# Hymba-style decoder layer, one core: where normalized columns leave from, when the t3 block is made, how many operands are loaded ahead

## The chip, the cores and the metric

One core of one Trainium2 chip runs the whole layer in one program. The metric is the device time of that program in microseconds (us), the median of several runs; lower is better. The engines are PE (matrix multiply, with PEld for its weight loads), DVE (VectorE), ACT (ScalarE), POOL (GpSimd) and SP, whose queue issues every DMA of the part spoken of here.

## What is computed

One decoder layer on 1024 tokens of width 1024, in float32. The change lies in its last half, the squared-ReLU MLP between two norms:

```python
x = x + jnp.concatenate([attn, conv], axis=-1) @ w_out[l]
h = rmsnorm(x, norm_ffn_g[l])
x = x + jnp.square(jax.nn.relu(h @ w_ffn_up[l])) @ w_ffn_down[l]
return rmsnorm(x, norm_final_g)
```

## The kernel before

Each float32 operand is split into a high part (ACT, L55) and a low part (DVE or POOL, L56), and a product is three passes of PE (L59 to L61). Each engine runs a queue of its own in order; outside the hand-ordered attention part the framework's scheduler sets the order of each queue, and each DMA is issued from SP's queue, on one of eight semaphores in turn. Tiles of one tag share a ring of buffers; who allocates the next one waits for the last readers and writers of the buffer that it gets.

**The second norm** (`norm_rows` and `norm_cols2`). For each of eight blocks of 128 tokens PE makes the last part of the output projection (`oc`), DVE adds it to the residual `x2[t]` (L815), SP stores `x2[t]` to `x2d` (L860), ACT squares and sums it into a buffer `xn` (L116), POOL makes the inverse root (L82, L83), DVE multiplies into `xn` (L145). One block later `norm_cols2` transposes `xn` on PE (L851, tile `n_t`), splits the columns into `h2h` and `h2l`, copies the columns once more on ACT (L854) and stores them to `hraw` in DRAM (L855). There are two `xn` buffers.

**The up projection.** Sixteen pairs of 128 hidden columns each. Pairs 0 and 1 are plain (`up_plain`): four products `up` of 24 matmuls over `h2h`/`h2l`, one for each half `e` of the columns and half `hf` of the tokens. Pairs 2 to 15 use seven products of half the size in place of eight (`up7`, tiles `u`), whose moving operands are sums of blocks of the columns: `t1s`, `t2s`, `t4s` (`make_moving`, from tiles `b` that are loaded back from `hraw`) and t3, the difference of two blocks of the second token half (`make_t3`, tiles `c`), which is written over the first four rows of `h2h[1]` and `h2l[1]`. The products of a pair run in the order 1, 5, 6, 2, 3, 7, 4. ACT copies the first two out of PSUM (L991, L992, tiles `us`); four PSUM tiles `two` go round. Results and their sums (`work_q`, `work_s`; L906, L907, L908, L914) are stored to `hid` in DRAM (L893).

**The down projection** has seven groups of seven products `dn` each, and an eighth whose products go straight into the final sums: group 0 takes the products in the order 1, 2, 3, 5, 6, 7, 4. A product needs a block of `hid` (tile `h`, one load) and a block of the weights (`b11`, `b21`, `b22`, `b12`, or the sums t1, t2 and b22 - b12 that POOL makes in `sums`), which `prep` splits into operands `d0..hi` and `d0..lo` (three buffers each). It has two halves of 12 matmuls; each half is added to an accumulator: `xe`, copied by ACT for group 0, or the residual `xr`, which is loaded back from `x2d` in four tiles (`reload_x2`). `xr0` takes the buffer of `work_q`, so its loads wait for the last store of the up projection. `begin_down`, in the middle of the last up pair, loads the operands of the first three products.

Of the kernel before, what the change touches and what calls it, by code (L numbers as in the profile page):

```python
# [5 lines left out]
F32 = mybir.dt.float32  # L6
F32R = mybir.dt.float32r
BF16 = mybir.dt.bfloat16
AF = mybir.ActivationFunctionType
# [5 lines left out]
P = 128  # L15
S = 1024
D = 1024
KT = D // P
# [9 lines left out]
HN = 512  # L28
# [5 lines left out]
def body(tc, x, norm_mix_g, w_in, b_forget, conv_dw_w, conv_dw_b, conv_ln_g, conv_ln_b,  # L34
# [3 lines left out]
    V, A, G, T, SP = nc.vector, nc.scalar, nc.gpsimd, nc.tensor, nc.sync  # L38
# [15 lines left out]
    def split(hi, lo, src, eng=V):  # L54
        A.activation(hi, src, AF.Copy)  # L55
        eng.tensor_tensor(lo, src, f32(hi), op=ALU.subtract)  # L56

    def mm3(ps, sh, sl, mh, ml, first, last):
        T.matmul(ps, sh, mh, start=first, stop=False)  # L59
        T.matmul(ps, sh, ml, start=False, stop=False)  # L60
        T.matmul(ps, sl, mh, start=False, stop=last)  # L61
# [7 lines left out]
    def ps_big(name):  # L69
        return psum.tile([P, 2 * HN], F32, tag="big", name=name, bufs=2)  # L70
# [666 lines left out]
    for t in range(NT):  # L737
        n = CV0 + CVS * t
# [23 lines left out]
    with tc.manual_schedule(engines={mybir.EngineType.PE}):  # L762
        for n in range(START, len(units) + 30):
# [4 lines left out]
            if 0 <= n < len(units):  # L768
                weighted_v(n, *prs.pop(n))
                h, hf, kt = units[n]  # L770
# [12 lines left out]
    x2 = [x2t[t // 2][:, t % 2, :] for t in range(NT)]  # L783
# [60 lines left out]
    hraw = dram.tile([KT, P, S], F32, name="hraw")  # L844
    x2d = dram.tile([NT, P, D], F32, name="x2d")

    def norm_cols2(t):
        xn = xns.pop(t)
        pt = ps_big(f"n2_{t}_t")
        for k in range(KT):  # L850
            T.transpose(pt[:, k * P:(k + 1) * P], xn[:, k * P:(k + 1) * P], ident)  # L851
        hf, c = t // 4, (t % 4) * P
        split(h2h[hf][:, :, c:c + P], h2l[hf][:, :, c:c + P], pt.rearrange("p (k n) -> p k n", k=KT))
        A.activation(xn, pt, AF.Copy)  # L854
        SP.dma_start(hraw[:, :, t * P:(t + 1) * P].rearrange("k p n -> p k n"), xn.rearrange("p (k n) -> p k n", k=KT))  # L855

    for t in range(NT):
        for hf in range(2):
# [6 lines left out]
    def ps_two(name):  # L865
        return psum.tile([P, 2, HN], F32, tag="two", name=name, bufs=4)
# [5 lines left out]
    def raw4(name):  # L872
        return rps[0].tile([P, 2, HN], F32, tag="raw4", name=name, bufs=8)

    def load_up(j):
        return load_w2(w_up_k[:, :, j * P:(j + 2) * P], f"up{j}", [P, KT, 2 * P])
# [7 lines left out]
    def up_half(p, w, e, hf, ps):  # L884
        sl = slice(e * P, (e + 1) * P)
        for k in range(KT):
            mm3(ps, w[0][:, k, sl], w[1][:, k, sl], h2h[hf][:, k, :], h2l[hf][:, k, :], k == 0, k == KT - 1)
        q = work["q"][:, e, hf, :]
        A.activation(q, ps, AF.Relu)
        V.tensor_tensor(q, ps, q, op=ALU.mult)  # L890

    def store(p, i, a):
        SP.dma_start(hid[i][p if i else p - NPAIR + 2], a)  # L893

    def sums_up(p, last):
        q, sm = work["q"], work["s"]
        a11, a21, a12, a22 = q[:, 0, 0, :], q[:, 0, 1, :], q[:, 1, 0, :], q[:, 1, 1, :]
        s1, s2, s3, s4 = [sm[:, i, :] for i in range(4)]
        plain = p >= NPAIR - 2
        if not last:  # L900
            store(p, 1, a11)
            store(p, 4, a22)
            if plain:
                store(p, 0, a21)
                return
            V.tensor_tensor(s1, a21, a22, op=ALU.add)  # L906
            V.tensor_tensor(s2, s1, a11, op=ALU.subtract)  # L907
            V.tensor_tensor(s3, a11, a21, op=ALU.subtract)  # L908
            for i, a in ((5, s1), (6, s2), (7, s3)):
                store(p, i, a)  # L910
        else:
            store(p, 2, a12)
            if not plain:
                V.tensor_tensor(s4, a12, s2, op=ALU.subtract)  # L914
                store(p, 3, s4)

    def up_plain(p, w, hfs):
        for e in range(2):
            for hf in hfs:
                up_half(p, w, e, hf, ps_two(f"up{p}{e}{hf}")[:, 0, :])  # L920
        sums_up(p, False)
        sums_up(p, True)

# [29 lines left out]
        mov[4] = [(t4[k // 2][:, k % 2, 0, :], t4[k // 2][:, k % 2, 1, :]) for k in range(4)]  # L953

    def tmp(name):
        return tp.tile([P, HN], F32, tag="tmp", name=name, bufs=6)

    def load_hraw(name, k, hf):
        t = tmp(name)
        SP.dma_start(t, hraw[k, :, hf * HN:(hf + 1) * HN])  # L960
        return t
# [10 lines left out]
    def make_t3(k):  # L972
        b12, b22 = load_hraw(f"c12_{k}", k, 1), load_hraw(f"c22_{k}", 4 + k, 1)
        G.tensor_tensor(b12, b22, b12, op=ALU.subtract)
        split(*mov[7][k], b12)
# [31 lines left out]
    SEQ0 = (1, 2, 3, 5, 6, 7, 4)  # L1007
# [6 lines left out]
    def wtile(g, name, dt=F32):  # L1014
        if "wr" not in pools_d:
            return raw4(f"{name}_{g}")
        return pools_d["wr"].tile([P, 2, HN], dt, tag="wr", name=f"{name}_{g}", bufs=9)

    def load_b(g, nm):
        e, c = BLK[nm]  # L1020
        d = groups.setdefault(g, {})
        wd = w_dn_k[:, 4 * g:4 * g + 4, :].rearrange("p (q e) n -> p e q n", e=2)
        d[nm] = wtile(g, "b" + nm)
        SP.dma_start(d[nm], wd[:, e, :, c * HN:(c + 1) * HN])

    def load_h(g, i):
        d = groups.setdefault(g, {})
        d[i] = raw4(f"h{i}_{g}")
        src = hid[i][2 * g:2 * g + 2] if i else hid[0]
        SP.dma_start(d[i], src.rearrange("q p n -> p q n"))  # L1030
# [20 lines left out]
    def pair_tiles(name):  # L1051
        return [wgt.tile([P, 2, 2, HN], F32R, tag=tg, name=f"{name}{tg}", bufs=3) for tg in ("hi", "lo")]

    def prep(g, i):
        d = groups[g]
        hi, lo = pair_tiles(f"d{g}{i}")
        w = d["w"][i] if "w" in d else d[{1: "11", 2: "21", 3: "22"}[i]]
        if i == 4:
            G.tensor_tensor(w, d["21"], w, op=ALU.subtract)
        split(hi[:, 0], lo[:, 0], d[i])  # L1060
        split(hi[:, 1], lo[:, 1], w, G if i in (1, 2) else V)
        return hi, lo

    NPL = 2
    uws = {0: load_up(0)}
# [7 lines left out]
    tp = pool("tp", "left")  # L1073
# [5 lines left out]
    def begin_down():  # L1079
        vp0.release()  # L1080
        vp1.release()
        rps.append(pool("rp", "right"))
        for nm, i in (("11", 1), ("21", 2), ("22", 3)):
            load_b(0, nm)
            load_h(0, i)
        ready[0] = prep(*steps[0])

    for p in range(NPAIR):
        if p + 1 < NPAIR:
            uws[p + 1] = load_up(2 * p + 2) if p + 1 < NPL else load_up7(p + 1)  # L1090
        if p < NPL:
            for k in range(2 * p, 2 * p + 2):
                make_moving(k)
            up_plain(p, uws.pop(p), range(2) if p else (1,))
        else:
            if p == NPL:
                for k in range(4):
                    make_t3(k)
            up7(p, uws.pop(p), begin_down if p == NPAIR - 1 else None)
    tp.release()  # L1100
    hp.release()
# [1 line left out]
    xp = pool("xp", "left")  # L1103
# [3 lines left out]
    x2 = []  # L1107
# [35 lines left out]
    for n in range(-1, len(steps)):  # L1143
        if n < 0:
            ready[1] = prep(*steps[1])
            load_b(0, "12")
            load_h(0, SEQ0[3])
            reload_x2(0)
            reload_x2(1)
            load_h(0, SEQ0[4])  # L1150
            reload_x2(2)
            reload_x2(3)
            for i in SEQ0[5:]:
                load_h(0, i)
            sums(0)
            continue
        g, i = steps[n]
        if n == 3:
            for h in range(2):
                V.tensor_tensor(acc_of(3, h), acc_of(3, h), acc_of(5, h), op=ALU.subtract)  # L1160
        if n % 7 == 4 and g + 1 < NG - 1:
            sums(g + 1)
        if n + AHEAD < len(steps):
            ready[n + AHEAD] = prep(*steps[n + AHEAD])
        if i == 1:
            load_group(g + 1)
        if n == len(steps) - 1:
            d = groups[NG - 1]
            ops = {}
            for x, y, name in ((1, "11", "sa"), (2, "21", "sb"), ("12", "22", "sc"), (0, 4, "sd")):  # L1170
                if name == "sc":
                    hi, lo = [[wtile(NG - 1, f"{name}{e}{k}", F32R) for k in range(2)] for e in "hl"]
                else:
                    hi, lo = pair_tiles(name)
                    hi, lo = [hi[:, 0], hi[:, 1]], [lo[:, 0], lo[:, 1]]
                for k, z in enumerate((x, y)):
                    split(hi[k], lo[k], d[z])
                    ops[z] = hi[k], lo[k]
        products(g, i, *ready.pop(n))

    fin = xp.tile([P, D], F32, name="gfin")
    SP.dma_start(fin, norm_final_g.partition_broadcast(P))

    def final(t):
        y = wgt.tile([P, D], F32, tag="raw", name=f"yo{t}", bufs=3)
# [56 lines left out]
```

## Time and profile before

| | us |
|---|---|
| median of 3 runs | 1184.75 |
| lowest and highest | 1181.86, 1185.16 |
| profiled execution, its own time | 1181.96 |
| its span in the trace | 1180.2 |
| PE busy in the span | 1128.8 (96%) |
| DVE, ACT, POOL busy | 905.4 (77%), 466.2 (40%), 461.1 (39%) |
| HBM traffic over the span | 138 GB/s |

A busy time counts an engine's instructions, not the waits between them. PE's clock is granted at one of two levels, and the mean of a stretch is given as a share of the higher one. A wait is put down to what ended it. A line such as L851 is a line of the kernel before.

### The profile page before, as it was taken

How to read it: one execution, taken by the hardware profiler on the slowest of the kernel's cores; microseconds unless marked ns; L12 is line 12 of the kernel's file. 1: busy time of each engine (PE TensorE's matmuls, PEld its weight loads, DVE VectorE, ACT ScalarE, POOL GpSimd, SP SyncE). 2: the span in 40 equal slices, each digit the busy share in tenths (PEclk: the TensorE clock that was granted, in tenths of full speed). 3: DMA queues.
4: the chain of work that ended last, by engine and by line, in shares of the span. 5: the costliest groups of instructions: out<-in, count | busy, mean ns of one | idle time of the engine just before them, and what ended most of it. 6: DMA issues, size and time to landing. Idle time of an engine off the chain costs nothing.

```text
span 1180.2 us, 15131 instructions
## 1 busy us (share of the span) xinstructions
PE 1128.8 (96%) x5455; PEld 918.7 (78%) x5455; DVE 905.4 (77%) x1155; ACT 466.2 (40%) x715; POOL 461.1 (39%) x358
## 2 busy tenths in 40 slices
PE   6999999989999999989799999999979999999997
PEld 6899888867677678867688888888858888888876
DVE  5399999577887764555887878787568888878994
ACT  6322443138788932353322222222324433333422
POOL 7113255027778520134543434433264333443011
PEclk9999999999999999998899999999989999999999
DMA  8021145773333243355544444444684554445003
GB/s 265 11 67 46 27 108 133 203 210 108 91 91 90 101 167 110 122 179 181 202 137 167 134 161 147 151 154 164 250 335 155 178 169 141 137 147 173 19 17 126
DMA packets 121779, 164.52 MB, mean 139 GB/s; under 512 B 9112, under 2 KB 66792, under 8 KB 121704
## 3 DMA queue, kind: packets, MB, share of 16 engines
q1 hardware_dynamic: 121704, 163.56, 43.4%
q8 instruction: 43, 0.70, 0.3%
q14 instruction: 32, 0.26, 0.1%
HBM read 114.67 MB, written 48.79 MB: 138 GB/s over the span
## 4 chain that ended last, share of the span: by engine, by line
PE 56%; DVE 7%; ACT 4%; issue 3%; DMA 3%; POOL 2%; SPq 0%; DVEq 0%; POOLq 0%; ACTq 0%
PE u L59 7%; PE u L60 7%; PE u L61 7%; PE dn L60 7%; PE dn L61 7%; PE dn L59 7%; DMA hraw<-n_xn 2%; PE op L59 1%; PE op L61 1%; PE op L60 1%; DVE xr L1138 1%; PE fin L59 1%; PE fin L61 1%; PE fin L60 1%; PE s L445 1%
## 5 line engine op out<-in xcount | busy, mean ns | idle before, releaser
L292 DVE SCALAR_TENSOR_TENSOR conv<-u,par,conv 128x1024 f32<-128x1024 f32 x108 | 133.7, 1279 | 1.7 <-ACT conv L287 1.3
L1138 DVE TENSOR_TENSOR xr<-dn,xr 128x1024 f32<-128x1024 f32 x56 | 68.0, 1219 | 35.9 <-PE dn L61 35.8
L56 POOL TENSOR_TENSOR pl<-pt,ph 128x512 fp32r<-128x512 f32 (+3 forms) x71 | 74.1, 1059 | 25.1 <-ACT ph L55 22.0
L935 POOL TENSOR_TENSOR ur<-ur 128x512 f32<-128x512 f32 x14 | 22.7, 1620 | 93.4 <-DVE ulo6a L56 7.4
L613 ACT ACTIVATE pt<-sT,ctok 128x512 f32<-128x512 f32 (+1 forms) x96 | 54.5, 585 | 10.9 <-PE sT L611 5.8
L989 DVE SCALAR_TENSOR_TENSOR work_q<-work_q 128x512 f32<-128x512 f32 x56 | 52.7, 942 | 1.0
L453 DVE CUSTOM_DVE_ANT_0 mj<-s,ck 128x512 bf16<-128x512 f32 (+2 forms) x64 | 37.4, 585 | 19.8 <-PE s L447 8.8
L988 DVE TENSOR_TENSOR work_q<-u,us 128x512 f32<-128x512 f32 x42 | 28.6, 681 | 26.9 <-PE u L61 26.9
L55 ACT ACTIVATE ph<-pt 128x512 fp32r<-128x512 f32 (+1 forms) x96 | 48.7, 531 | 0.6
L1138 DVE TENSOR_TENSOR xe<-dn,xe 128x1024 f32<-128x1024 f32 x36 | 42.8, 1212 | 4.0 <-PE dn L61 4.0
L82 POOL TENSOR_SCALAR rs_tmp<-n_ss 128x1 f32<-128x1 f32 x16 | 5.6, 353 | 94.8 <-ACT n_xn L116 88.1
L59 PE MATMUL qk<-hTh,wh_qk 128*128 128x512 f32 x96 | 39.0, 406 | 0.4 <-DVE m L453 0.4
L60 PE MATMUL qk<-hTl,wh_qk 128*128 128x512 f32 x96 | 37.9, 395 | 0.0
L61 PE MATMUL qk<-hTh,wl_qk 128*128 128x512 f32 x96 | 37.8, 394 | 0.0
L445 PE MATMUL s<-ks,q 128*128 128x512 f32 (+2 forms) x96 | 36.8, 389 | 1.0 <-DVE m L453 0.9
L633 PE MATMUL av<-pl,v 128*65 128x512 f32 (+1 forms) x96 | 32.5, 339 | 3.9 <-POOL pl L56 2.4
L61 PE MATMUL v<-wh_v,hTl 128*128 128x260 f32 x128 | 36.1, 282 | 0.0
L60 PE MATMUL v<-wl_v,hTh 128*128 128x260 f32 x128 | 36.1, 282 | 0.0
L59 PE MATMUL v<-wh_v,hTh 128*128 128x260 f32 x128 | 36.0, 281 | 0.0
L631 PE MATMUL av<-ph,v 128*65 128x512 f32 (+1 forms) x96 | 35.3, 368 | 0.1
L930 POOL TENSOR_TENSOR ur<-ur 128x512 f32<-128x512 f32 x14 | 24.5, 1750 | 25.3 <-DVE up2l L56 2.5
L608 PE MATMUL sT<-q,ks 128*128 128x512 f32 (+1 forms) x96 | 33.6, 350 | 0.0
(1315 smaller groups left out, 3897.8 us busy)
## 6 DMA issues: line engine op xcount, KB each, us to landing
h<-hid SPq DMA_DIRECT2D x53, 512.0 KB
b<-in_w_ffn_down SPq DMA_DIRECT2D x32, 512.0 KB
ur<-in_w_ffn_up SPq DMA_DIRECT2D x56, 256.0 KB
hid<-work_s SPq DMA_DIRECT2D x56, 256.0 KB
hid<-work_q SPq DMA_DIRECT2D x50, 256.0 KB
xp<-in_x SPq DMA_DIRECT2D x8, 512.0 KB
qstack<-qk SPq DMA_DIRECT2D x32, 128.0 KB
kstack<-qk SPq DMA_DIRECT2D x32, 128.0 KB
```

What stands on the lines that cost most here:

```text
L55: A.activation(hi, src, AF.Copy)
L56: eng.tensor_tensor(lo, src, f32(hi), op=ALU.subtract)
L59: T.matmul(ps, sh, mh, start=first, stop=False)
L60: T.matmul(ps, sh, ml, start=False, stop=False)
L61: T.matmul(ps, sl, mh, start=False, stop=last)
L292: V.scalar_tensor_tensor(dst, u[:, k:k + S], tap_w(c, k), cell[0], op0=ALU.mult, op1=ALU.add)
L445: T.matmul(ps[:, :w], d["q2"][:, i * P:(i + 1) * P], d["ks"][:, b0:b1], start=True, stop=b1 < n)
L453: V.tensor_tensor_reduce(junk[:, :w], ps[:, :w], d["ck"][:, b0:b1], op0=ALU.subtract, op1=ALU.max, scale=1.0, scalar=d.pop("m0") if b0 els ...
L613: A.activation(pt[:, :w], ps[:, :w], AF.Exp, bias=ctok[:, h * NT + kt:h * NT + kt + 1])
L631: T.matmul(av[:DH + 1, o0:], v1, ph[:, :w], start=kt == ORDER[hf][0], stop=False)
L989: V.scalar_tensor_tensor(dst, dst, 0.0, dst, op0=ALU.max, op1=ALU.mult)
L1138: V.tensor_tensor(a, ps, a, op=ALU.add)
```

## The change

In `norm_cols2` the copy of the columns goes into the residual tile `x2[t]` in place of `xn`, and the store to `hraw` leaves from there. In `up_plain` the token half is the outer loop, pair 1 takes the second half first, and `make_t3` is called between its halves; it was called at the start of pair 2. The ring of `tmp` tiles (`b`, `c`, `us`, `uu`) has 7 buffers, not 6. `begin_down` loads b12 and the `h` block of the fourth product too, in the ring that its other loads use. The final norm's gain is loaded at step 14 of the down projection's loop.

```diff
-        A.activation(xn, pt, AF.Copy)
-        SP.dma_start(hraw[:, :, t * P:(t + 1) * P].rearrange("k p n -> p k n"), xn.rearrange("p (k n) -> p k n", k=KT))
+        A.activation(x2[t], pt, AF.Copy)
+        SP.dma_start(hraw[:, :, t * P:(t + 1) * P].rearrange("k p n -> p k n"), x2[t].rearrange("p (k n) -> p k n", k=KT))
...
-        for e in range(2):
-            for hf in hfs:
+        for hf in hfs:
+            for e in range(2):
                 up_half(p, w, e, hf, ps_two(f"up{p}{e}{hf}")[:, 0, :])
+            if (p, hf) == (NPL - 1, 1):
+                for k in range(4):
+                    make_t3(k)
...
-        return tp.tile([P, HN], F32, tag="tmp", name=name, bufs=6)
+        return tp.tile([P, HN], F32, tag="tmp", name=name, bufs=7)
...
             load_b(0, nm)
             load_h(0, i)
+        load_b(0, "12")
+        load_h(0, SEQ0[3])
         ready[0] = prep(*steps[0])
...
-            up_plain(p, uws.pop(p), range(2) if p else (1,))
+            up_plain(p, uws.pop(p), (1, 0) if p else (1,))
         else:
-            if p == NPL:
-                for k in range(4):
-                    make_t3(k)
...
             ready[1] = prep(*steps[1])
-            load_b(0, "12")
-            load_h(0, SEQ0[3])
...
+        if n == 14:
+            fin = xp.tile([P, D], F32, name="gfin")
+            SP.dma_start(fin, norm_final_g.partition_broadcast(P))
...
-    fin = xp.tile([P, D], F32, name="gfin")
-    SP.dma_start(fin, norm_final_g.partition_broadcast(P))
```

How the queues stand then, at three places (lines behind the first edits are up to three higher in the changed kernel).

ACT, in the second norm from block 4's split on (`n_t` transposed columns, `x_4825` the residual of blocks 6 and 7, `uhi2a` weights of pair 2). Before:

```order
L55 ACTIVATE h2h_5106<-n_4_t 128x8x128
L55 ACTIVATE uhi2a<-ur_5711 128x1024
L854 ACTIVATE n_4_xn<-n_4_t 128x1024
L55 ACTIVATE uhi2a<-ur_5712 128x1024
L55 ACTIVATE h2h_5106<-n_5_t 128x8x128
L889 ACTIVATE work_q<-up_5523 128x512
L116 ACTIVATE n_6_xn,n_6_ss<-x_4825 128x1024
L854 ACTIVATE n_5_xn<-n_5_t 128x1024
L889 ACTIVATE work_q<-up_5550 128x512
L116 ACTIVATE n_7_xn,n_7_ss<-x_4825 128x1024
```

Now:

```order
L854 ACTIVATE x_4824<-n_4_t 128x1024
L116 ACTIVATE n_6_xn,n_6_ss<-x_4825 128x1024
L55 ACTIVATE up2h<-up2r_5604 128x1024
L55 ACTIVATE up2h<-up2r_5608 128x1024
L55 ACTIVATE h2h_5106<-n_5_t 128x8x128
L55 ACTIVATE uhi2a<-ur_5711 128x1024
L854 ACTIVATE x_4824<-n_5_t 128x1024
L116 ACTIVATE n_7_xn,n_7_ss<-x_4825 128x1024
L55 ACTIVATE uhi2a<-ur_5712 128x1024
L55 ACTIVATE h2h_5106<-n_6_t 128x8x128
```

The square of block 7 (L116, `n_7_xn`) stood behind block 5's copy and two copies of `work_q`; it stands behind block 5's copy and one weight split, and the copies (L854) write `x`, not `xn`.

SP, around the loads of the t3 block (`c`; L893 stores to `hid`: `hid_5506` block 4, `hid_5507`, `hid_5508`, `hid_5509` the sums, `hid_5503` block 1). Before, from the store of pair 0's second sum on:

```order
L893 DMA hid_5508<-work_s 128x512
L893 DMA hid_5505<-work_s 128x512
L960 DMA c_0_5910<-hraw 128x512
L893 DMA hid_5503<-work_q 128x512
L960 DMA c_0_5912<-hraw 128x512
L960 DMA c_1_5917<-hraw 128x512
L960 DMA c_1_5919<-hraw 128x512
L960 DMA c_2_5924<-hraw 128x512
L960 DMA c_2_5926<-hraw 128x512
L960 DMA c_3_5931<-hraw 128x512
L893 DMA hid_5509<-work_s 128x512
L960 DMA c_3_5933<-hraw 128x512
```

Now, from the first `c` load on:

```order
L963 DMA c_0_5822<-hraw 128x512
L893 DMA hid_5508<-work_s 128x512
L893 DMA hid_5505<-work_s 128x512
L963 DMA c_0_5824<-hraw 128x512
L963 DMA c_1_5829<-hraw 128x512
L963 DMA c_1_5831<-hraw 128x512
L963 DMA c_2_5836<-hraw 128x512
L893 DMA hid_5506<-work_q 128x512
L963 DMA c_2_5838<-hraw 128x512
L893 DMA hid_5507<-work_s 128x512
L963 DMA c_3_5843<-hraw 128x512
L963 DMA c_3_5845<-hraw 128x512
```

The first load of c_0 stands two places earlier, ahead of pair 0's last two sums, and the next four one place earlier; the loads of c_3 stand where they were or one place later, behind pair 1's stores of block 4 and of its first sum.

SP, at the start of the down projection (`b_0` and `h_0` operands of group 0, `h_1` of group 1, `xr` the residual). Before, from the seventh load on:

```order
L1030 DMA h_0_7892<-hid_5507 128x2x512
L1030 DMA h_0_7900<-hid_5508 128x2x512
L893 DMA hid_5503<-work_q 128x512
L1030 DMA h_0_7908<-hid_5509 128x2x512
L1182 DMA gfin<-in_norm_final_g 128x1024
L893 DMA hid_5510<-work_q 128x512
L1113 DMA xr_7902<-x2d 128x1024 x2
L1030 DMA h_0_7910<-hid_5506 128x2x512
L1113 DMA xr_7905<-x2d 128x1024
L893 DMA hid_5506<-work_q 128x512
L1024 DMA b_0_7890<-in_w_ffn_down 128x2x512
L1113 DMA xr_7905<-x2d 128x1024
```

Now, from the seventh load on:

```order
L1027 DMA b_0_7803<-in_w_ffn_down 128x2x512
L1033 DMA h_0_7805<-hid_5507 128x2x512
L893 DMA hid_5503<-work_q 128x512
L1033 DMA h_0_7900<-hid_5508 128x2x512
L1160 DMA gfin<-in_norm_final_g 128x1024
L893 DMA hid_5510<-work_q 128x512
L1115 DMA xr_7902<-x2d 128x1024 x2
L1033 DMA h_0_7908<-hid_5509 128x2x512
L1115 DMA xr_7905<-x2d 128x1024
L893 DMA hid_5506<-work_q 128x512
L1115 DMA xr_7905<-x2d 128x1024
L1033 DMA h_0_7910<-hid_5506 128x2x512
```

b12 (`b_0_7890` before, `b_0_7803` now) stood eleven transfers further back than it stands now; the `h_0` loads are each one to five places later. The load `gfin` of the final gain has not moved.

PE, same place, the first matmul of each half of products 6, 7 and 4, with what it waits for. Before:

```order
L59 MATMUL dn_8089<-d06hi 128x512 [waits DVE_49,Activation_49]
L59 MATMUL dn_8103<-d06hi 128x512 [waits DVE_49]
L59 MATMUL dn_8123<-d07hi 128x512 [waits DVE_49,Activation_49]
L59 MATMUL dn_8137<-d07hi 128x512 [waits Activation_49]
L59 MATMUL dn_8157<-d04hi 128x512 [waits Activation_49]
L59 MATMUL dn_8171<-d04hi 128x512 [waits DVE_49]
```

Now:

```order
L59 MATMUL dn_8089<-d06hi 128x512 [waits DVE_49,Activation_49]
L59 MATMUL dn_8103<-d06hi 128x512 [waits Activation_49]
L59 MATMUL dn_8123<-d07hi 128x512 [waits Activation_49]
L59 MATMUL dn_8137<-d07hi 128x512 [waits Activation_49]
L59 MATMUL dn_8157<-d04hi 128x512 [waits DVE_49]
L59 MATMUL dn_8171<-d04hi 128x512 [waits DVE_49]
```

The second half of product 6 waited for DVE and now waits for ACT; the halves of product 7 wait for ACT in both, and product 4's first half now waits for DVE.

## Rows read from the trace of the kernel before

**Rows 1.** Busy time by stretch: PE, PEld, DVE, ACT, POOL, then granted clock, DMA share, GB/s

```profile
500.00:560.00 60.00, 52.54 (x237) 42.68 (x237) 34.52 (x32) 26.69 (x36) 23.99 (x21) 0.91 0.56 175
...
640.00:680.00 40.00, 40.00 (x176) 32.81 (x175) 33.52 (x40) 10.18 (x13) 15.24 (x10) 1.00 0.46 155
...
840.00:880.00 40.00, 33.51 (x137) 26.82 (x135) 26.06 (x22) 13.61 (x14) 19.42 (x9) 0.91 1.03 387
...
530.00:534.00 4.00, 1.71 (x8) 1.56 (x8) 2.42 (x2) 1.51 (x2) 0.74 (x2) 0.50 0.01 2
```

**Rows 2.** Waits of PE, whole span: total us, times, longest us

```profile
PE n_t L851 <- DVE n_xn L145: 5.9, 2, 4.3
...
PE u L59 <- ACT us L991: 6.4, 1, 6.4
...
PE dn L60 <- DVE d05lo L56: 4.4, 1, 4.4
...
PE dn L59 <- ACT d05hi L55: 2.1, 1, 2.1
```

**Rows 3.** Timeline of PE, 524 to 541 us: start, us, instruction [idle before <-releaser]

```profile
526.92 1.07 PE L851 MATMUL n_t<-ident,n_xn 128*128 128x128 f32 x8 [1.57 <-DVE n_xn L145]
...
532.29 1.94 PE L851 MATMUL n_t<-ident,n_xn 128*128 128x128 f32 x8 [4.30 <-DVE n_xn L145]
...
538.90 0.63 PE L59 MATMUL up<-h2h,up0h 128*128 128x512 f32 x1
```

**Rows 4.** Chain that ended last, 520 to 546 us: start, us, what

```profile
525.49 3.20 DMA hraw<-n_xn
...
530.86 1.28 DVE n_xn L145
...
536.58 1.03 ACT n_xn L854
...
537.63 3.41 DMA hraw<-n_xn
...
541.98 3.34 DMA b<-hraw
```

**Rows 5.** Timeline of POOL, 470 to 600 us

```profile
518.73 2.29 POOL L932 TENSOR_TENSOR ur<-ur,ur 128x512 f32<-128x512 f32 x1
```

**Rows 6.** Timelines of DVE, SP and PE, 546 to 586 us

```profile
546.34 1.22 DVE L56 TENSOR_TENSOR t1s<-b,t1s 128x512 fp32r<-128x512 f32 x1 [9.79 <-ACT t1s L55]
...
571.34 0.68 DVE L56 TENSOR_TENSOR t2s<-b,t2s 128x512 fp32r<-128x512 f32 x1
...
576.52 0.32 SPq L960 DMA_DIRECT2D c<-hraw  x1
...
578.68 0.40 PE L61 MATMUL u<-t2s,ulo2a 128*128 128x512 f32 x1
...
585.45 0.80 PE L59 MATMUL u<-h2h,uhi2a 128*128 128x512 f32 x1 [6.37 <-ACT us L991]
```

**Rows 7.** Timelines of SP, POOL, PE and ACT, 840 to 893 us

```profile
840.34 1.78 SPq L1030 DMA_DIRECT2D h<-hid  x3
...
852.75 0.38 SPq L1024 DMA_DIRECT2D b<-in_w_ffn_down  x1
...
866.78 1.03 SPq L1113 DMA_DIRECT2D xr<-x2d  x2
...
862.34 2.47 POOL L1046 TENSOR_TENSOR t<-b,b 128x1024 f32<-128x1024 f32 x1 [15.01 <-DMA b<-in_w_ffn_down]
...
865.19 0.39 PE L61 MATMUL dn<-d03hi,d03lo 128*128 128x512 f32 x1
...
881.74 0.47 PE L59 MATMUL dn<-d06hi 128*128 128x512 f32 x1 [1.41 <-DVE xr L1138]
...
892.75 0.39 PE L59 MATMUL dn<-d04hi 128*128 128x512 f32 x1
...
884.75 1.03 ACT L1136 ACTIVATE xe<-dn 128x1024 f32<-128x1024 f32 x1 [2.37 <-PE dn L61]
```

## The prediction

> **What bounds the kernel now.** I read the busy times by stretch first, then PE's list of waits, then each wait's place in the timelines and in the chain that ended last. In the long middle of the squared-ReLU stage PE is busy for 40.00 of 40 us at full clock, so nothing that shortens another engine's work there is worth anything; where the change lies it is busy for 52.5 of 60 and 33.5 of 40 us, at a mean granted clock of 0.91 [rows 1]. The list of waits names three places [rows 2]. **N**: PE waits 5.9 us for the second norm's last blocks, `n_xn`. **T**: in the first seven-product pair it waits 6.4 us for ACT's copy `us`. **D**: at the start of the down projection it waits 2.1 and 4.4 us inside product 5, and 1.4 behind it [rows 7]. A wait of over 4 us costs twice, because the clock falls to its lower level behind it: after 4.30 us idle eight transposes take 1.94 us, where the same eight took 1.07 behind a wait of 1.57 us, and matmuls last 0.63 us [rows 3], at a granted clock of 0.50, 1.2 of 2.4 GHz [rows 1].
>
> **N, the column copy leaves from the residual's buffer.** The square of block t writes an `xn` buffer that before was also the source of the transfer to `hraw`, so ACT could not start it until that transfer had landed: 3.20 us for block 5's, and only then square, `rsqrt` and the multiply by the gain at 530.86 [rows 4]. Now the buffer's last reader is PE's transposes. By the order, block 7's square stands behind block 5's copy and ahead of the second `uhi2a`. What still delays its `rsqrt` is POOL's order: it stands behind L932, which ends at 521.0 [rows 5]. With the `rsqrt` under 1 us and the multiply at 1.28 us [rows 4] the block is ready near 523. PE wants it at 526.4: before, its matmuls had run out 1.57 us ahead of 526.92, and block 6's transposes add 1.07 [rows 3]. So both waits go, 5.9 us. With them goes the slow spell: 0.87 us on the transposes and about 1.4 on seven matmuls that started 0.2 us further apart. N gives 8.1 us; the 1.1 us in which PE waits for the split of block 7 stays (if even that drops the clock, N gives 6). The copy must now wait until `x2d[t]` is stored; that store stands in SP's queue as soon as the block is summed, ahead of its square, transposes and splits, and a transfer of that size takes 3.4 us [rows 4]: nothing.
>
> **T, the t3 block in the second plain pair.** The order of halves costs PE nothing, the matmuls are the same. The wait at 578.68 lasts until 585.45 because the PSUM tile it needs is freed by `us`, which stands on ACT behind all four t3 splits and `uhi3a`. It still stands there. So T ends a fixed chain after the last `c` load: 576.52 to 585.45 is 8.9 us [rows 6]. When is that load issued now? In SP's queue it is now behind pair 1's store of `s1`, hence behind DVE. DVE needed from 546.34 to 572.0 for 20 instructions, 1.28 us each [rows 6]. The run starts when the last `hraw` transfer and a `b` load have landed, and that transfer waits for block 7's copy, 536.58 [rows 4]. The copy follows the last transposes, 4.3 us after their start, 3.4 with fast transposes, so now at 529.8: the run starts 6.8 us earlier, at 539.6. To that `s1` there are 21 instructions, 26.9 us: 566.5. The two last `c` loads follow, the second behind the splits of c_0 and b_3, 2 to 4 us: 569 to 571. PE's product then starts at about 579, while PE, 8.1 us early, is there at 571.0: a wait of 8 us in place of 6.4. T takes back 1.6 us. Best end: DVE runs ahead, the wait is gone with its slow spell (12 matmuls by 0.2 us, 2.4), a gain of 8.8. Worst: the loads are 4 us later still.
>
> **D, b12 and h5 loaded with the first three.** Before, b12 stood eleven transfers later in SP's queue, issued at 852.75; the place that it has now was reached in the batch of three at 840.34. POOL's sums began on it at 862.34, 9.6 us after its issue [rows 7], with the DMA engines full, 387 GB/s [rows 1]. Issued now at about 841 it lands by 851, t1 (2.47 us [rows 7]) is there by 854, and the splits of product 5 end near 859. The h transfers behind it move back by one, 1.35 us each at that rate, and are asked for much later. PE asks at 865.4. The waits of 2.1 and 4.4 us and the slow spell go. But see what comes next: products 2, 3 and 5 hold three of four PSUM tiles until `xr0` has landed, so products 6 and 7 share one tile. By the new waits in PE's queue each of their last three halves waits for ACT to empty the one before: 1.03 us, begun 0.2 us after the matmuls [rows 7], 3.7 in sum. Product 6 waits for DVE's add as before, 1.4 us, up to 3 when POOL's next sums run beside it; I take 2.2. From 865.4 to 892.75 there were 27.3 us for three products; the last two took 11.0 without a wait [rows 7], so 16.5 for three and 10.8 lost. 5.9 are lost now. D gives 4.9 us, 2.5 to 6.
>
> **The rest.** The final gain's load is in the same place in SP's queue as before, behind h6 or h7: nothing. The seventh `tmp` buffer only lets loads go earlier. Pair 1's stores to `hid`, now partly behind `c` loads, are read back only in the down projection. Later groups have the same order.
>
> **Sum**: 8.1 - 1.6 + 4.9 = 11.4 us. The profiled execution took 1181.96 us (span 1180.2); it is 2.8 below the median of the three runs shown, 1184.75. The same gain from the median gives 1173.4 us.
>
> **Rivals.**
> - **T's wait vanishes** (21.8 us gained, 1163.0). It needs the last `c` load some 8 us earlier than I put it. For it: seven buffers, and the loads stand earlier than pair 1's last stores. Against: two stores of DVE's sums stand ahead of them. 0.15.
> - **T eats N.** If POOL and DVE get in each other's way more, with four t3 sums more in the same run, the last load comes 5 us later: 1178.4. 0.14.
> - **The clock at D.** Four gaps of 1.2 to 2.2 us within 17 us lie in products 6 and 7. In the rows a gap of 1.41 us before 881.74 or of 1.57 before 526.92 is followed by full speed [rows 3, 7], so I charge nothing for them. If the clock did fall, 48 matmuls at 0.2 us are 9.6 us, and the sum is 1.8: 1183.0. 0.07. The Trainium skill, "TensorE: Matmul & The Clock Gate", section "A second HAM failure mode: psum-queue depth-cycling", describes just that: PE idling a little between groups while it cycles through PSUM banks, and a clock that goes up and down. By the rows above short gaps do not do it; four in a row no row of before shows.
> - **Slower, by `xr0`.** Its two loads, issued at 866.78 [rows 7], now have three more 512 KB transfers ahead, 1.35 us each at the rate of [rows 1], so they land near 880.5 instead of 876.4. Product 4 needs their adds by about 888, so they decide from 885 on, each us one for one. Slower than no change by over 0.3% needs a landing after 900. Nothing points to 14 transfers more. 0.03, at 1188 or above.
> - **Nothing moves** (1184.8), if another wait of an `n_xn` kept its place. 0.04.
>
> **How the numbers follow.** The forecast has 0.57, its own range is 1170 to 1180 (N 6 to 8.1, T -4 to 0, D 2.5 to 6). Taking in the vanished wait, with 2 us for what I don't know of it, and the case in which T eats N, the range is 1161 to 1181. A measurement of this kernel can tell about 0.3%, 3.6 us, from no change. Faster by more: the forecast, the vanished wait and T eating N, 0.86; within: the clock and nothing, 0.11; slower: 0.03.
>
> **What would show it.** N right: no wait of PE for `n_xn`, full clock from 526 to 535. T: a wait of PE in pair 2 of 6 to 10 us, in one or two pieces, ending near 579; below 3 us my DVE run is wrong. D: no wait for `d05lo`; four short waits, one for DVE's add to `xr`, three for ACT's copies to `xe`, at full clock; product 4 some 5 us nearer to product 3. If PE waits there for `xr0`, or its clock falls, D is wrong. The forecast is wrong if the gain is under 4 or over 16 us.

## The result, and the profile after

The changed kernel took 1175.21 us (median of four runs, 1172.95 to 1175.83), where the kernel before took 1184.76 in the same session: 0.9922 of it, with a 95% interval of 0.9902 to 0.9942, or 9.5 us less. Forecast were 1173.4 and a range of 1161 to 1181. Run once more beside its variants (below), the change gave 0.9934 [0.9919, 0.9948], 7.8 us. The sum was near; two of its three terms were not.

The busy times by stretch, in the columns of [rows 1], of the second norm, then of the start of the down projection and of two pieces of it:

```profile
500.00:560.00 60.00, 58.12 (x272) 47.87 (x271) 40.32 (x36) 26.90 (x36) 29.41 (x23) 1.00 0.64 199
...
840.00:880.00 40.00, 31.64 (x126) 24.74 (x125) 31.53 (x19) 15.24 (x16) 20.77 (x7) 0.87 0.94 358
867.90:873.20 5.30, 5.30 (x12) 3.76 (x12) 3.14 (x2) 0.00 (x0) 0.92 (x1) 0.50 0.88 324
874.40:885.60 11.20, 8.91 (x37) 6.75 (x38) 5.94 (x5) 3.95 (x5) 2.46 (x1) 1.00 0.49 166
```

Around the second norm PE is busy for 58.1 of 60 us at full clock, where it was 52.5 at 0.91 [rows 1]. At the start of the down projection it is busy for 31.6 of 40 us against 33.5, but that window began 9 us ahead of the first product before and begins with it now, so the marks further down compare better. The list of PE's waits, against [rows 2]:

```profile
PE dn L59 <- DVE xr L1140: 6.1, 1, 6.1
PE u L59 <- DVE work_q L890: 3.9, 1, 3.9
...
PE dn L59 <- ACT xe L1138: 3.3, 3, 1.1
...
PE u L59 <- ACT us L994: 0.8, 1, 0.8
```

No wait for `n_xn` is left, none for `d05hi` or `d05lo`. In their places stand one of 6.1 us for DVE's add to `xr` and three of 1.1 us for ACT's copies to `xe`; the wait in pair 2 is in two pieces. Where they lie, from PE's timeline (start, us, instruction, idle before):

```profile
527.75 1.04 PE L851 MATMUL n_t<-ident,n_xn 128*128 128x128 f32 x8
529.90 0.49 PE L59 MATMUL up<-h2h,up0h 128*128 128x512 f32 x1 [1.11 <-ACT h2h L55]
531.16 0.50 PE L60 MATMUL up<-h2l,up0h 128*128 128x512 f32 x1 [0.77 <-DVE h2l L56]
...
573.25 0.54 PE L59 MATMUL u<-t2s,uhi2a 128*128 128x512 f32 x1 [3.85 <-DVE work_q L890]
573.59 0.63 PE L60 MATMUL u<-t2s,uhi2a 128*128 128x512 f32 x1
...
578.64 0.50 PE L59 MATMUL u<-h2h,uhi2a 128*128 128x512 f32 x1 [0.79 <-ACT us L994]
...
861.36 0.39 PE L61 MATMUL dn<-d05hi,d05lo 128*128 128x512 f32 x1
867.89 0.76 PE L59 MATMUL dn<-d06hi 128*128 128x512 f32 x1 [6.14 <-DVE xr L1140]
868.45 0.63 PE L60 MATMUL dn<-d06lo,d06hi 128*128 128x512 f32 x1
...
874.46 0.49 PE L59 MATMUL dn<-d06hi 128*128 128x512 f32 x1 [1.11 <-ACT xe L1138]
...
878.58 0.50 PE L59 MATMUL dn<-d07hi 128*128 128x512 f32 x1 [1.11 <-ACT xe L1138]
...
882.71 0.50 PE L59 MATMUL dn<-d07hi 128*128 128x512 f32 x1 [1.11 <-ACT xe L1138]
```

Behind 867.89 twelve matmuls run at the lower clock (0.50 in the stretch from 867.9, 0.63 us each, 0.43 apart where 0.23 is usual, 2.4 us). Behind the gaps of 1.11 us the clock stays at 1.00.

To set the two executions side by side I take four marks, the first matmuls of pairs 2 and 3 (`uhi2a`, `uhi3a`) and of the products 1 and 4 of group 0 (`d01hi`, `d04hi`), from the views of these tiles (instructions of one kind, shortest/median/longest ns, first to last start). Before:

```profile
L59 PE MATMUL u<-h2h,uhi2a x8: 389/508/796, 570.6 to 589.5; 128*128 128x512 f32 x8
L59 PE MATMUL u<-h2h,uhi3a x8: 389/389/395, 599.0 to 609.4; 128*128 128x512 f32 x8
...
L59 PE MATMUL dn<-d01hi x8: 389/389/389, 849.1 to 853.9; 128*128 128x512 f32 x8
L59 PE MATMUL dn<-d04hi x8: 389/389/389, 892.8 to 897.5; 128*128 128x512 f32 x8
```

After:

```profile
L59 PE MATMUL u<-h2h,uhi2a x8: 389/389/500, 563.7 to 580.8; 128*128 128x512 f32 x8
L59 PE MATMUL u<-h2h,uhi3a x8: 389/389/395, 589.6 to 600.0; 128*128 128x512 f32 x8
...
L59 PE MATMUL dn<-d01hi x8: 389/389/389, 839.8 to 844.5; 128*128 128x512 f32 x8
L59 PE MATMUL dn<-d04hi x8: 389/389/389, 885.6 to 890.3; 128*128 128x512 f32 x8
```

So pair 2 begins 6.9 us earlier, takes 25.9 us instead of 28.4 (2.5 less; pair 3, which waits for nothing, takes 19.3), and the down projection needs 45.8 us to product 4 instead of 43.7 (2.1 more). The changed execution came out of the attention part 1.6 us late: the same matmul `av` of the attention starts at 415.82, before at 414.19, ahead of all that was changed. N is therefore 8.5 us, T 2.5 and D -2.1 in this pair of profiles, 8.9 in sum. The span fell by 7.1 us (1180.2 to 1173.1), the 8.9 less those 1.6 us, within rounding.

### The profile page after: what moved, and what is told of

The parts are those of the page before. It is cut to its first block, busy times and chain, and to the rows that moved or that the text cites. A ratio compares the mean times of both kernels' runs of the same rounds, so it can differ in the third digit from the quotient of the medians.

```text
span 1173.1 us, 15113 instructions
## 1 busy us (share of the span) xinstructions
PE 1126.2 (96%) x5455; PEld 916.0 (78%) x5455; DVE 918.3 (78%) x1155; ACT 466.9 (40%) x715; POOL 462.6 (39%) x358
## 5 line engine op out<-in xcount | busy, mean ns | idle before, releaser
L613 ACT ACTIVATE pt<-sT,ctok 128x512 f32<-128x512 f32 (+1 forms) x96 | 54.4, 584 | 11.4 <-POOL pl L56 5.3
L992 DVE SCALAR_TENSOR_TENSOR work_q<-work_q 128x512 f32<-128x512 f32 x56 | 56.4, 1006 | 1.0
L991 DVE TENSOR_TENSOR work_q<-u,us 128x512 f32<-128x512 f32 x42 | 28.6, 681 | 25.9 <-PE u L61 25.8
L631 PE MATMUL av<-ph,v 128*65 128x512 f32 (+1 forms) x96 | 35.3, 368 | 0.1
L244 ACT ACTIVATE qk<-qk 128x512 fp32r<-128x512 f32 x16 | 9.5, 592 | 60.9 <-PE qk L61 51.8
```

What stands on the lines that cost most here:

```text
L613: A.activation(pt[:, :w], ps[:, :w], AF.Exp, bias=ctok[:, h * NT + kt:h * NT + kt + 1])
L631: T.matmul(av[:DH + 1, o0:], v1, ph[:, :w], start=kt == ORDER[hf][0], stop=False)
L992: V.scalar_tensor_tensor(dst, dst, 0.0, dst, op0=ALU.max, op1=ALU.mult)
```

## The experiments

The kernels ran in three groups (four rows of the table each), each group on one chip with the kernel before. Ratios are to that, with 95% intervals. "Pair 2" and "D" are the lengths between the marks above, in the profiled execution (before 28.4 and 43.7, changed 25.9 and 45.8).

| kernel | median, us | ratio | pair 2 | D |
|---|---|---|---|---|
| n_only | 1176.93 | 0.9957 [0.9944, 0.9970] | 29.8 | 44.7 |
| no_t | 1175.95 | 0.9952 [0.9939, 0.9965] | 29.3 | 45.0 |
| no_d | 1171.62 | 0.9917 [0.9904, 0.9930] | 26.5 | 43.5 |
| seq | 1165.61 | 0.9862 [0.9846, 0.9878] | 26.2 | 34.7 |
| after2 | 1174.91 | 0.9934 [0.9919, 0.9948] | 26.2 | 44.7 |
| no_pool1 | 1170.34 | 0.9898 [0.9883, 0.9913] | 25.9 | 40.4 |
| no_sub | 1164.85 | 0.9861 [0.9842, 0.9879] | 26.0 | 37.7 |
| t_mid | 1175.76 | 0.9940 [0.9924, 0.9956] | - | 45.3 |
| seq2 | 1165.77 | 0.9847 [0.9830, 0.9864] | 26.0 | 35.3 |
| seq_sq | 1166.12 | 0.9849 [0.9833, 0.9865] | 27.4 | 35.4 |
| seq_sq_mid | 1164.86 | 0.9843 [0.9823, 0.9864] | - | 35.5 |
| no_n | 1182.99 | 0.9999 [0.9988, 1.0011] | 27.8 | 45.7 |

### The parts alone and taken back

`n_only`, the kernel before with the first edit alone:

```diff
-        A.activation(xn, pt, AF.Copy)
+        A.activation(x2[t], pt, AF.Copy)
```

(and the store to `hraw` from `x2[t]`).

> The kernel before with the first edit alone (the columns' copy and its store leave from the residual's tile). Theory (three places add up; in the two profiles N gave 8.5 us, T 2.5, D -2.1): N alone gives 7.5 to 8.5 us, about 1176.5 where the kernel before has 1184.75, no wait of PE for n_xn, and T's wait for the copy us stays between 5 and 8 us. Rival (N alone is eaten at T, since the t3 chain ends when it ended): T's wait grows to 10 us or more and the gain is under 5 us, above 1179.5.

It gave 5.1 us (0.43% of 1181.7), between the two. Pair 2 begins at 563.1, 7.5 us earlier than before, so N itself is there (0.6 of it is an earlier end of the attention part; the other 6.9 are N with a slow spell soon behind the short gaps there, as in the last section). Two later waits say where the rest went:

```profile
579.38 0.80 PE L59 MATMUL u<-h2h,uhi2a 128*128 128x512 f32 x1 [7.79 <-ACT us L991]
...
867.83 0.79 PE L60 MATMUL dn<-d05lo,d05hi 128*128 128x512 f32 x1 [5.55 <-DVE d05lo L56]
```

The wait for `us` grew by 1.4 us (6.37 before [rows 6]) and the one for `d05lo` by 1.15 (4.40 [rows 2]). The first is the 1.6 us that the prediction charged to T, nearly: it belongs to N without the t3 edit. The second lies in a stretch whose code is that of the kernel before, so D differs by 1.0 us (44.7 against 43.7) between two profiles without any change to it.

`no_n`, the changed kernel with that edit undone.

> The changed kernel with the columns' copy and its store back in the xn buffer. Theory (N takes 8 us off the second norm, whatever T and D do): two waits of PE for n_xn of 1.5 and 4.3 us and the slow clock behind the second are back, the place where pair 2 begins is 8 us later, and the whole is 5 to 8 us slower than the changed kernel, 1179 to 1182. Rival (the t3 block of the second plain pair would have hidden N's wait, since DVE's run and not PE sets pair 2): pair 2 then begins later but waits less, and the whole is under 3 us slower.

The gain is gone altogether, 0.9999, a little more than was expected. PE's list of waits has `n_xn` again. Pair 2 begins at 570.0, 6.3 us later than in the changed kernel where 8 was expected, but this execution left the attention part 2.2 us earlier (its last matmul `av` at 414.27 against 416.52), so from there it is 8.5. Pair 2 takes 27.8 us, and D takes 45.7:

```profile
PE n_t L851 <- DVE n_xn L145: 5.6, 2, 4.3
PE u L59 <- DVE work_q L890: 5.3, 2, 4.7
```

The first theory holds. The other edits together are worth nothing without N: in the profiles T wins 0.6 us there, D loses 2.0.

`no_t`, the changed kernel with the loop over the halves and the call of `make_t3` as before:

```diff
-        for hf in hfs:
-            for e in range(2):
+        for e in range(2):
+            for hf in hfs:
...
+            if p == NPL:
+                for k in range(4):
+                    make_t3(k)
```

> The changed kernel with the order of the plain pairs' halves and the place of the t3 block as before; seven tmp buffers stay. Theory (T gave 2.5 us in the profiles): 1177 to 1179, with one wait of PE of 5 to 8 us for the copy us in pair 2. Rival (the prediction's T, a loss of 1.6 us): 1173 to 1174, faster than the changed kernel.

0.9952 against 0.9922 and 0.9934 for the whole change: 2 to 3.5 us slower, with intervals that overlap. One wait of 7.15 us for `us` is back and pair 2 takes 29.3 us. In the profiles the lengths of pair 2 do not overlap: 28.4 to 29.8 in the three without the t3 edit, 25.9 to 26.5 in the seven that have it with N and with the square on DVE. T is a gain, so the rival, which was the prediction's own term, falls.

`no_d`, with b12 and the fourth `h` loaded where they were:

```diff
-        load_b(0, "12")
-        load_h(0, SEQ0[3])
         ready[0] = prep(*steps[0])
...
             ready[1] = prep(*steps[1])
+            load_b(0, "12")
+            load_h(0, SEQ0[3])
```

> The changed kernel with b12 and the fourth h block loaded where the kernel before loads them. Theory (at the start of the down projection the change lost 2.1 us): 1172 to 1174, 2 us faster than the changed kernel's 1175.2, and product 4 stands 27.3 us behind product 3's end against 29.7. Rival (the prediction's D, a gain of 4.9, hidden in the scatter of the two profiled executions): 1180, 5 us slower than the changed kernel.

0.9917, not slower than the change: the prediction's 4.9 us are excluded. The waits of 2.1 and 4.4 us for `d05hi` and `d05lo` are back, the one of 6.1 is gone, and D takes 43.5 us. The five profiles that contain the edit and nothing else in D (changed, after2, no_t, t_mid, no_n) have 44.7 to 45.8, 45.3 in the mean; the three without it (before, n_only, no_d) have 43.5 to 44.7, 44.0 in the mean. In the runs the loss, 0.6 to 2 us, is not apart from zero: the intervals overlap. That the edit gained nothing is shown; that it lost 1 to 2 us is likely and no more.

`after2` is the changed kernel again.

> The changed kernel itself once more, so that it stands beside the others on the same chip. It should give 0.992 of the kernel before, and the same waits of PE: 3.9 us in pair 2 for DVE, 6.1 us in the down projection for DVE's add to xr, three of 1.1 us for ACT's copies.

The waits in D are the same to 0.02 us, but behind the one of 6.12 six matmuls run slow and not twelve, 1.1 us less. Those in pair 2 are 2.5 and 2.3 us, not 3.9 and 0.8, and the time is 7.8 us below before.

### Why the early b12 won nothing

First, what DVE does in the changed kernel while PE waits from 861.7 to 867.9, and POOL beside it:

```profile
857.49 2.51 DVE L56 TENSOR_TENSOR d07lo<-h,d07hi 128x1024 fp32r<-128x1024 f32 x1
859.92 3.40 DVE L1163 TENSOR_TENSOR xr<-xr,xr 128x1024 f32<-128x1024 f32 x1
863.25 3.36 DVE L56 TENSOR_TENSOR d07lo<-b,d07hi 128x1024 fp32r<-128x1024 f32 x1
866.53 1.21 DVE L1140 TENSOR_TENSOR xr<-dn,xr 128x1024 f32<-128x1024 f32 x1
```

```profile
859.22 3.02 POOL L1049 TENSOR_TENSOR t<-b,b 128x1024 f32<-128x1024 f32 x1 [0.31 <-DMA b<-in_w_ffn_down]
862.32 3.21 POOL L1050 TENSOR_TENSOR t<-b,t 128x1024 f32<-128x1024 f32 x1
865.48 3.33 POOL L1051 TENSOR_TENSOR b<-b,b 128x1024 f32<-128x1024 f32 x1
```

The add at 866.53 empties product 5's second half, the only PSUM tile not held for `xr0`, and product 6 needs it. Product 5 ended at 861.7, but the add stands behind the subtraction L1163 and a split, which take 3.4 us each beside POOL's sums for group 1 (1.21 without them, as the next run shows). The Trainium skill, "SBUF — State Buffer", section "SBUF: two separate sides", says that VectorE, with two operands in SBUF, and GpSimd lock the same pair of ports for a whole instruction, the other waiting. The rows agree: 3.4 us with two SBUF operands, and 1.21 for the add at 866.53, which runs beside POOL too but reads one operand from PSUM.

`no_pool1` takes POOL's three sums for group 1 away:

```diff
         d = groups[g]
+        if g == 1:
+            d["w"] = {1: d["11"], 6: d["22"], 7: d["12"], 5: d["11"], 4: d["12"], 3: d["22"], 2: d["21"]}
+            return
```

> The changed kernel without POOL's three sums for group 1 of the down projection, which run beside DVE from 859 to 869 us (products of group 1 then take unsummed blocks of the weights; the arithmetic of that group is not the layer's). Theory (the add that frees product 6's PSUM tile is late because two DVE instructions ahead of it take 3.4 us each beside POOL, 1.2 alone): they take 1.2 us, the add starts 4 us earlier, PE's wait falls from 6.1 to 1.4 to 2 us, the clock stays up (2.4 us): 6 to 7 us faster than the changed kernel. The three waits of 1.1 us for ACT stay. Rival (the add waits for xr1 to xr3 landing, or for the transfers that fill the DMA engines): the wait stays above 4 us and the time within 2 us of the changed kernel.

DVE's rows, then PE's:

```profile
859.10 1.21 DVE L1166 TENSOR_TENSOR xr<-xr,xr 128x1024 f32<-128x1024 f32 x1
860.23 1.21 DVE L56 TENSOR_TENSOR d07lo<-b,d07hi 128x1024 fp32r<-128x1024 f32 x1
861.37 1.21 DVE L1143 TENSOR_TENSOR xr<-dn,xr 128x1024 f32<-128x1024 f32 x1
```

```profile
862.72 0.47 PE L59 MATMUL dn<-d06hi 128*128 128x512 f32 x1 [1.80 <-DVE xr L1143]
...
866.81 0.50 PE L59 MATMUL dn<-d06hi 128*128 128x512 f32 x1 [1.11 <-ACT xe L1141]
```

The two instructions take 1.21 us, the wait 1.80, the clock stays up, as the theory said. The gain over after2 is 4.6 us, not 6 to 7: with product 6 earlier a fourth wait of 1.11 us for ACT's copy appeared, before product 4, and after2's slow spell had cost 1.1 us less than the 2.4 counted on.

`no_sub` takes L1163 away:

```diff
-        if n == 3:
-            for h in range(2):
-                V.tensor_tensor(acc_of(3, h), acc_of(3, h), acc_of(5, h), op=ALU.subtract)
```

> The changed kernel without DVE's subtraction of the residual's second half from its first for group 0 (acc 3 less acc 5; the output then holds that term twice). It takes 3.4 us off DVE's queue just ahead of the add that frees product 6's tile, and frees product 5's first half from the wait for xr0. Theory (DVE's queue, and three tiles held for xr0): PE's wait for the add falls to 2.8 us or less, and two tiles, not one, go round in products 6 and 7, so that the waits for ACT's copies go too: 6 to 10 us faster than the changed kernel. Rival (ACT's copies alone bound products 6 and 7, whatever DVE does): the add's wait goes, the three waits of 1.1 us stay, 3 to 6 us.

The wait is 2.85 us, no wait for ACT's copies is left, D takes 37.7 us, and the kernel is 10.1 us faster than after2 by the medians (8.6 by the ratios), at the top of what was expected; 7.0 of it is D by the two profiles, the rest is not accounted for. The edit does two things at once, but `no_pool1` did one of them alone, and there the copies' waits stayed: DVE's queue made the long wait, and the tiles held until DVE's adds to `xr0` made the three others.

`seq` gives PSUM back without leaving work out: products 6 and 7, which ACT empties, run before 3 and 5.

```diff
-    SEQ0 = (1, 2, 3, 5, 6, 7, 4)
+    SEQ0 = (1, 2, 6, 7, 3, 5, 4)
...
-        for nm, i in (("11", 1), ("21", 2), ("22", 3)):
+        for nm, i in (("11", 1), ("21", 2)):
             load_b(0, nm)
             load_h(0, i)
         load_b(0, "12")
+        load_b(0, "22")
+        load_h(0, SEQ0[2])
         load_h(0, SEQ0[3])
```

> The changed kernel with the products of group 0 in the order 1, 2, 6, 7, 3, 5, 4, and the first loads in that order, so that only one PSUM tile, not three, waits for xr0 while products 6 and 7 run. Theory (the loss at D is PSUM: three tiles held for xr0, and the fourth freed by a DVE add that stands late in DVE's queue): the waits of 6.1 us for DVE's add and of 3.3 us in three for ACT's copies go, and the slow clock's 2.4 us with the first; 8 to 11 us faster than the changed kernel, 1164 to 1167. Rival (the transfers bound this stretch, DMA engines full until product 6): the same wait comes back as one for an h block, b block or xr0, 1173 to 1178.

0.9862, and 0.9847 when run again: some 9 us faster than the change, as the theory had it. From product 1 to product 4 PE is busy for 33.2 of 34.7 us (stretch, sum, PE, granted clock, DMA share, GB/s):

```profile
838.50:873.20 34.70, 33.15 (x145) 1.00 1.04 396
```

The DMA engines are as full as before (396 GB/s), so the transfers did not bound this stretch. POOL's sums still slow DVE here (3.41 us for a split at 863.09), but no tile waits for it. `seq2` is the same kernel as a base for the next two.

> The kernel with group 0 in the order 1, 2, 6, 7, 3, 5, 4 once more, as the base for the next two on the same chip: 0.986 of the kernel before, 1164 to 1167, and 35 us from product 1's first matmul to product 4's.

It took 1165.77 us.

### What is left of T

`t_mid` calls `make_t3` inside the first seven-product pair, behind its third product:

```diff
-            if (p, hf) == (NPL - 1, 1):
-                for k in range(4):
-                    make_t3(k)
...
-            up7(p, uws.pop(p), begin_down if p == NPAIR - 1 else None)
+            up7(p, uws.pop(p), begin_down if p == NPAIR - 1 else t3_all if p == NPL else None)
```

> The changed kernel with the t3 block called inside the first seven-product pair, behind its third product, so that ACT's copies us stand ahead of the t3 splits. Theory (what is left of T, 6.9 us of pair 2's 25.9, is the two waits for tiles that are freed behind the t3 splits on ACT and DVE, and the slow clock behind them): both waits go, 4 to 7 us faster than the changed kernel, 1168 to 1171 where that has 1175.2. Rival (the t3 block itself is late: its loads are now behind all stores of pair 1): PE waits 4 us or more at product 7 or 4 or in pair 3 for c's splits, and the gain is under 2 us or a loss.

The rival in the main: no difference from after2. The waits at products 6 and 2 are gone, but another stands at product 7, the first that needs t3, though of less than the rival's 4 us,

```profile
582.95 0.50 PE L59 MATMUL u<-h2h,uhi2b 128*128 128x512 f32 x1 [2.87 <-ACT h2h L55]
```

and pairs 2 and 3 take 44.5 us together, against 45.2 in the changed kernel. The t3 block is late in every place tried.

`seq_sq` takes work off DVE, on top of `seq`:

```diff
         A.activation(q, ps, AF.Relu)
-        V.tensor_tensor(q, ps, q, op=ALU.mult)
+        A.activation(q, q, AF.Square)
```

> The kernel of the new product order, and in the plain pairs ACT makes the square too (relu, then Square of the result), where DVE multiplied. Theory (what is left of T comes from DVE, which works without a pause from 541 to 582 us, slowed by POOL, so that the t3 block and the tile of product 6 come late): five DVE instructions of 0.7 to 1.2 us leave that run, the tile is freed by ACT's relu alone, and pair 2 takes 21 to 23.5 us, not 26.2: 3 to 5 us faster than the new order alone. Rival (ACT's own order, where the relu stands behind t3 splits, or the c loads' place in SP's queue sets the end): pair 2 stays at 25.5 us or more and the time within 1 us.

A miss: 1166.12, no gain, pair 2 longer at 27.4 us. PE's row, then ACT's:

```profile
573.41 0.79 PE L59 MATMUL u<-t2s,uhi2a 128*128 128x512 f32 x1 [5.36 <-ACT work_q L889]
```

```profile
569.74 0.63 ACT L55 ACTIVATE h2h<-c 128x512 fp32r<-128x512 f32 x1 [4.09 <-POOL c L977]
572.25 0.63 ACT L55 ACTIVATE h2h<-c 128x512 fp32r<-128x512 f32 x1 [1.88 <-POOL c L977]
572.78 0.58 ACT L889 ACTIVATE work_q<-up 128x512 f32<-128x512 f32 x1
```

The relu that frees the tile stands on ACT behind t3 splits, which wait for POOL's differences of `c`, as the rival said. In the changed kernel the tile was freed by DVE's multiply; taking the multiply off DVE only moved the hold to ACT's order.

`seq_sq_mid` has both edits.

> As the kernel before this one, and the t3 block called inside the first seven-product pair. In the changed kernel that moved PE's wait from products 6 and 2 to product 7 and won 0.8 us over pairs 2 and 3. Theory (DVE's run was what made the t3 block late there too): pairs 2 and 3 take 40 to 42 us together, where 38.0 would be without a wait, 1 us or so faster than the version without it. Rival (the loads of c, now behind the stores of pair 1, set the end): PE still waits 2 to 4 us at product 7, and the time is the same or 1 to 2 us more.

Its wait at product 7 is 1.07 us and pairs 2 and 3 take 41.2 us, as expected, 4 less than in the changed kernel. Its time, 1164.86, is not apart from seq2's. The profiled execution began pair 2 at 568.6, 5 us later than seq2's, and that lag comes from the attention part, ahead of every edit: its last matmul `av` starts at 419.54 against 414.39, with a granted clock of 0.91 from 260 to 300 us and 0.96 from 300 to 340, where seq2 has 1.00. Why the clock fell there, and what T can still give, stays open.

## Why the prediction was right, and where it was not

**The total** fell inside the range and near the forecast because two errors of opposite sign met: T came out 4.1 us better than its term and D 7.0 worse, and N 0.4 better. That is luck. Against the sum of 11.4 stand 8.9 us of the profiles. What was taken for nothing, the seventh `tmp` buffer and the later load of the final gain, no run tries alone.

**N: right.** No wait for `n_xn`, full clock, and 8.5 us against 8.1. `no_n` shows it from the other side, 8 to 9 us slower than the change. In `after2` and `n_only`, where the clock fell behind the short gaps, N was 6.9. The wait of 1.11 us for block 7's split stayed, as written.

**T: the mark was right, the term was not.** Product 2 was forecast to begin near 579 and began at 578.64, behind two waits of 4.6 us in sum, where the sign given was 6 to 10. The mark owes 1.6 us to the late end of the attention part: counted from pair 2's first matmul, product 2 began 14.9 us behind it, as before (585.45 less 570.6), where 16.5 was forecast (579 less 562.5, which is 570.6 less N's 8.1). That is 1.6 of the 4.1 us: the chain that ends T was shorter than forecast. The other 2.6 lie behind product 2. The failing step is "a wait of 8 us in place of 6.4": the wait that came was shorter, and the step set a wait against a wait and left out the slow clock behind each. Before, that spell came after the `us` it had waited for and added 2.8 us (28.4, less 19.2 for pair 3 in the same profile, less 6.37). Now it falls on product 6, ahead of `us`, in time that PE would have spent waiting. Compared as pair lengths the term is +2.5. The rivals "T's wait vanishes" and "T eats N" did not come; what `n_only` lost there shows that pair 2 would have taken back 1.4 us without the edit.

**D: wrong, no gain at all and by the profiles a loss.** The first half held: b12's early load removed 2.1 and 4.4 us for `d05`, and the three waits for ACT's copies came as forecast, 3.3 us for 3.7. The failing step is "Product 6 waits for DVE's add as before, 1.4 us, up to 3 when POOL's next sums run beside it; I take 2.2". The add itself took 1.21 us. What the step did not count was the queue ahead of it, two DVE instructions of 3.4 us. In the kernel before both were done while PE waited for `d05lo` until 872.81 or worked on product 5 behind it (DVE's rows before; L1160 there is the subtraction L1163):

```profile
868.26 3.36 DVE L1160 TENSOR_TENSOR xr<-xr,xr 128x1024 f32<-128x1024 f32 x1
...
873.82 1.21 DVE L56 TENSOR_TENSOR d07lo<-b,d07hi 128x1024 fp32r<-128x1024 f32 x1
```

When that wait went, PE met them at product 6. `no_pool1` and `no_sub` shorten that queue in two ways, and the wait falls to 1.80 and 2.85 us. The wait of 6.14 then cost 2.4 us more by the clock (1.1 less in `after2`).

**The rivals at D.** The clock did fall there, but behind the one long wait, not for the reason of the rival, several short gaps. The Trainium skill ("TensorE: Matmul & The Clock Gate", section "A second HAM failure mode: psum-queue depth-cycling") tells of a kernel whose clock went down and up because PE idled briefly between groups while it cycled through PSUM banks. In D such gaps did not do it: the three of 1.11 us in the changed kernel, and one of 1.80 with four of 1.11 behind it in `no_pool1`, have a granted clock of 1.00 throughout. Behind gaps no longer than these it fell elsewhere, as the last section shows. The slower rival by `xr0` did not come. Three tiles stayed held until DVE's adds from 880.65 on, and at the end not for the transfer. The DMA engines moved 10 GB/s from 878 to 882.4, where they had moved 391 at 872, so the transfers asked for by 872, `xr0`'s among them (issued at 859.35), had landed by 878. What the adds stood behind in DVE's queue was a split for group 1, which waited for ACT:

```profile
879.51 1.22 DVE L56 TENSOR_TENSOR d11lo<-h,d11hi 128x1024 fp32r<-128x1024 f32 x1 [8.47 <-ACT d11hi L55]
880.65 2.35 DVE L1140 TENSOR_TENSOR xr<-dn,xr 128x1024 f32<-128x1024 f32 x2
```

Before, these adds stood ahead of that split. How much of the three waits for ACT's copies is this order, and how much `xr0`'s own time, no run tells apart.

## What to carry to other kernels

A wait that is removed lets its engine run into the next thing that the wait had covered: before an operand is loaded earlier, list on the engine that frees the buffers what stands ahead of the freeing instruction, at its slowed duration. Count a stretch from mark to mark, slow clock and all, not wait against wait. And when products need accumulators whose adds come late, order them so that few of the PSUM tiles are held for those: here that was worth twice what the better load was meant to win, and `seq` (1165.61 us) is faster than both kernels.

## What was not expected of the hardware

The clock can fall or stay behind the same gaps in two executions of one program. In `after2`, at the place where the changed kernel ran on at full speed (531.16 above), the gaps are the same to 0.02 us, and nine matmuls run slow, 1.8 us (PE's timeline, then granted clock 0.67 in the stretch's row):

```profile
529.88 0.49 PE L59 MATMUL up<-h2h,up0h 128*128 128x512 f32 x1 [1.11 <-ACT h2h L55]
531.14 0.64 PE L60 MATMUL up<-h2l,up0h 128*128 128x512 f32 x1 [0.77 <-DVE h2l L56]
531.58 0.63 PE L61 MATMUL up<-h2h,up0l 128*128 128x512 f32 x1
```

```profile
530.00:534.00 4.00, 3.23 (x8) 0.67 0.80 244
```

`seq` and `seq2`, again one program with the same two gaps, differ in the same way: 1.00 and 0.70 from 530 to 535 us. So the prediction's "if even that drops the clock, N gives 6" is a matter of the execution. It is likely a part of the 2 to 6 us by which runs of one kernel differ here, as is the end of the attention part (its last matmul starts between 414.3 and 419.5 in these profiles), and it bounds what a single pair of profiles can tell.
